# Hybrid encoder trunk: the pooled group's loads and splits as a step of their own, and the last division beside the Fourier tables

## The chip, the cores and the metric

The kernel runs on one core of a Trainium2 chip. The metric is the time of one execution in microseconds (us), as the device reports it; a kernel's figure is the median over its runs. The profile is one further execution under the hardware profiler, with a time and a span of its own.

## The reference

A trunk of two layers (DEPTH = 2) over 1040 positions (16 meta tokens ahead of 1024) and 1024 channels. Per layer:

```python
hn = rmsnorm(h, norm_w[i])
proj = einsum("bld,de->ble", hn, w_in[i])       # one projection for four head groups
y_pool = multiscale_pool(u_pool, ...) * silu(g_pool)
y_fft  = fourier_mix(u_fft, fourier_w[i]) * silu(g_fft)
y_ssd  = ssd_mixer(xbc, z, dt_raw, ...)         # bidirectional scan
y_att  = gqa_axial(q, k, v, ...) * silu(g_attn)
h = h + einsum("ble,ed->bld", concatenate([y_pool, y_fft, y_ssd, y_att]), w_out[i])
```

The pooled group is a centred mean over 2, 4, 8 or 16 positions minus the token, a linear map per group of 128 channels, a scale and the gate. The attention is softmax attention of 8 query heads on 2 key heads.

## The kernel before

Everything is kept transposed: channels on the 128 partitions, positions along the free dimension, in three chunks of 348, 346 and 346 (`CH`, line 26; in the last layer the first chunk drops the 16 meta tokens and has 332). A matrix product of full precision is three matmuls of rounded operands: `split` (lines 127 to 129) makes a high part on ScalarE and a low part on VectorE, `mm3` (lines 131 to 134) multiplies them.

**The order of the work** is written as generators. Each `yield` ends a step, and `weave` (lines 983 to 992) draws steps from several streams: each stream has a weight n, and the stream whose next step has the smallest (done + 0.5) / n goes next. So a stream with s steps and weight n ends at about s / n of the weave. The planner of the framework then makes each engine's queue from this order: it may put an instruction ahead of others where its own estimate says that its inputs and buffers are there. An engine runs its queue in that order, and so does SP, which issues nearly all transfers.

**Buffers.** `big` tiles (30 of 128 x 1056 f32, lines 97 and 98) hold nearly all that lives long; `sm("s")` is a set of four 128 x 348 tiles (lines 100 to 104) for rows on their way between DRAM and the engines. PSUM has tags "mm", "sc", "pv", "xx", and three spare banks, which `phase["spare"]` gives to one tag or another (lines 114 to 122): ('sc', 'sc', 'mm') while attention runs, ('xx', 'mm', 'xx') from the Fourier tables on. So "xx" has one bank before and three after that switch.

**Around the change** (`hybrid_trunk`, lines 1044 to 1072), once per layer:

- `att_main(l, s, t)` (line 642) is the attention of head pair t: per chunk three batches of three key blocks; `score` (line 648) makes two matmuls per head, an exponential on ScalarE and a running sum on GpSimd or VectorE (line 668); `weigh` (line 671) multiplies the batch before by the values; `divide` (line 682) sums over keys by a matmul (line 687), takes Ln and Exp, and scales (lines 691 to 693). A gate projection of 12 steps lies within. For t = 3 it has 51 steps: the last three are the last `weigh`, the last `divide`, and the gate's SiLU with product and store (lines 712 to 719).
- `pool_group` (line 357) makes the pooled rows of group g and stores them to DRAM, `s.md["p"]` (line 400): 34 steps in all.
- `fill` is a chain of projections whose results go to DRAM; at t = 3, 117 of its steps are left, the last of them those of the gate Z.
- `outproj(l, s, g, mixed, ...)` (line 330) is the output projection of head group g, 8 blocks of columns by 3 chunks, 24 steps. Its first line calls `mixed()`; for the pooled group that is `load_mixed(s, "p")` (line 320): 12 transfers through the `sm("s")` tiles (line 325), each split into `big` tiles (line 326). Each step reads the residual rows (line 338), multiplies, adds on VectorE (line 352) and stores them (line 353).
- For t = 3 the weave has three streams: attention with weight 50, the pooled groups with weight 60, and the filler with the first five out-projection steps behind it, with weight 1.5 x (108 + 5) = 169.5.
- Then the attention's pool of tiles is closed, the scan's pool is opened, and the Fourier stage begins: `fft_tables` (line 404) loads the weights `fw` (line 415; for i = 1 and 3 without their first row, so 127 rows), adds them (lines 423 and 427) and multiplies them with a cosine table (lines 432 and 434); `fft_inner` (line 443) and `fft_outer` follow. Further out-projection steps are woven in. The scan's loads (`ssd_load`, line 830, and `z` of `ssd_fin`, line 945) take tiles of the scan's pool.

Of the kernel before, what the change touches and what calls it, by code (L numbers as in the profile page):

```python
# [52 lines left out]
def hybrid_trunk(ctx: ExitStack, tc: tile.TileContext, io, out, depth=DEPTH):  # L53
# [25 lines left out]
    FB = (5, 5, 4, 1, 4, 1, 6, 9)  # L79
    GA = (22, 23, 22, 13)  # L80
    PS, WF = 60, 1.5
    FK = 3
    FN = (9, 17, 17, 16, 27)
    PC = 8 // GK
    TP = 0
# [2 lines left out]
    LS = 38  # L88
# [4 lines left out]
    def nm(s):  # L93
        uid[0] += 1
        return f"{s}{uid[0]}"

    def big(dt=F32):
        return bigp.tile([128, SLOT], dt, name=nm("big"), tag="big", bufs=NBIG)
# [3 lines left out]
    def sm(tag="n", dt=F32):  # L102
        pool = phase["p"] if tag == "q" else smp
        return pool.tile([128, 348], dt, name=nm("sm" + tag), tag="sm" + tag, bufs=phase["q"] if tag == "q" else SMB[tag])

    phase = {}
# [20 lines left out]
    def split(hi, lo, src):  # L127
        nc.scalar.copy(hi, src)  # L128
        nc.vector.tensor_tensor(lo, src, f(hi), op=ALU.subtract)  # L129
# [63 lines left out]
    def wsplit(raws, cols=128):  # L193

        r = []
        for raw in raws:
            wh = wp.tile([128, 4, 128], F32R, name=nm("wh"), tag="wh", bufs=WB[1])
            wl = wp.tile([128, 4, 128], F32R, name=nm("wl"), tag="wl", bufs=WB[1])
            split(wh[:, :, :cols], wl[:, :, :cols], raw)
            r += [(wh[:, k, :cols], wl[:, k, :cols]) for k in range(4)]  # L200
        return r

    def wraw(src, cols=128):
        w = wp.tile([128, 4, 128], F32, name=nm("wr"), tag="wr", bufs=WB[0])
        nc.sync.dma_start(w[:, :, :cols], src)
        return w[:, :, :cols]
# [109 lines left out]
    def whole(m):  # L316

        return lambda s, i, k, ci: m[i][k][:, s.ch[ci][0]:sum(s.ch[ci])]

    def load_mixed(s, key):  # L320
        m = [[big(F32R) for _ in range(4)] for _ in range(2)]
        for c0, cw in s.ch:
            for k in range(4):
                t = sm("s")
                nc.sync.dma_start(t[:, :cw], s.md[key][k, :, c0:c0 + cw])
                split(m[0][k][:, c0:c0 + cw], m[1][k][:, c0:c0 + cw], t[:, :cw])
        return whole(m)


    def outproj(l, s, g, mixed, src, dst, chunks=(0, 1, 2), pool=False, sink=None):  # L330

        part = mixed()
        for d in range(8):
            w = wsplit([wraw(io["w2"][l, g, d])])
            for ci in chunks:
                c0, cw = s.ch[ci]
                ht = sm("s")[:, :cw]
                nc.sync.dma_start(ht, src(d, ci)[:, -cw:])
                p = ps("mm")
                for k in range(4):  # L340
                    mm3(p[:, :cw], *w[k], part(s, 0, k, ci), part(s, 1, k, ci), k == 0, k == 3)
                o = ht
                if sink is not None:
                    if len(sink) == d:
                        sink.append(big())
                    o = sink[d][:, c0:c0 + cw]
                if pool:
                    t = sm("s")[:, :cw]
                    nc.scalar.copy(t, p[:, :cw])
                    nc.gpsimd.tensor_tensor(o, ht, t, op=ALU.add)  # L350
                else:
                    nc.vector.tensor_tensor(o, ht, p[:, :cw], op=ALU.add)  # L352
                nc.sync.dma_start(dst(d, ci)[:, -cw:], o)
                yield
# [623 lines left out]
    def run(*gens):  # L978
        for g in gens:
            for _ in g:  # L980
                pass

    def weave(*streams):

        st = [[iter(g), n, 0] for g, n in streams]
        while st:
            x = min(st, key=lambda x: (x[2] + 0.5) / x[1])
            x[2] += 1
            if next(x[0], StopIteration) is StopIteration:
                st.remove(x)  # L990
            else:
                yield

    def chain(*gens):
        for g in gens:
            yield from g
# [6 lines left out]
    def by_rows(x, off=0):  # L1003
        return lambda d, ci: x[d * 128:d * 128 + 128, max(CH[ci][0] - off, 0):sum(CH[ci]) - off]
# [9 lines left out]
    hsrc = by_rows(io["xT"])  # L1014
    s = layer(0)
# [7 lines left out]
    for l in range(depth):  # L1023
        last = l == depth - 1
        scope = ExitStack()
        phase["p"], phase["q"] = scope.enter_context(tc.tile_pool(name=nm("attp"), bufs=1)), 4
        phase["spare"] = SPARE[0]
        conv = iter([ssd_conv(l, s, t) for t in range(8)])
        parts = {"U": spill(l, s, T_UP, 4, "u"), "P": spill(l, s, T_GP, 4, "p", s.ch), "D": chain(spill_dt(l, s), ssd_dt(l, s)), "F": spill(l, s, T_GF, 4, "f", s.ch),
                 "Z": spill(l, s, T_Z, 4, "z", s.ch), "R": fft_proj(l, s)}  # L1030
        fill = chain(*[parts[x] if x in parts else next(conv) for x in FO])
        for g, shape in (("a", [4, 128, L]), ("p", [4, 128, L]), ("r", [4, 128, HALF + 1]), ("ny", [1, HALF + 1])):
            s.md[g] = drp.tile(shape, F32, name=nm("md"))
        s.md["x"] = drp.tile([8, 128, L], F32, name=nm("md"))
        kv = att_kv(l, s)
        if l == 0:
            run(prenorm(l, s, 0), weave((islice(kv, 2 * PC + 2), 2 * PC + 2), (prenorm(l, s, 1), 6)), weave((islice(kv, 2 * PC + 2), 2 * PC + 2), (prenorm(l, s, 2), 6)))
        else:
            run(weave((islice(kv, 4 * PC + 4), 4 * PC + 4), (prenorm(l, s, 2), 6)))
        s.h = None  # L1040
        run(weave((kv, 2 * PC + 4), (islice(fill, FK * PC), FK * PC)))
        phase["spare"] = SPARE[1]
        run(weave((chain(att_q(l, s, 0), att_max(l, s, 0)), 3 * PC + 6 + 18), (islice(fill, FN[0] * PC), FN[0] * PC)))
        for t in range(4):
            if t < 3:
                side = [att_q(l, s, t + 1), att_max(l, s, t + 1)]
            else:
                side = [pool_group(l, s, g) for g in range(4)]
            n = FN[t + 1] * PC
            if t < 3:  # L1050
                run(weave((att_main(l, s, t), LS + 3 * PC), (chain(*side), 20 + 3 * PC + 6), (islice(fill, n), n)))
        d0, d1, d2 = [hidden() for _ in range(3)]
        fill2 = chain(outproj(l, s, 0, lambda: load_mixed(s, "p"), hsrc, d0), outproj(l, s, 1, lambda: s.fm, d0, d2), outproj(l, s, 3, lambda: s.am, d2, d1, pool=True))
        run(weave((att_main(l, s, 3), LS + 3 * PC), (chain(*side), PS), (chain(fill, islice(fill2, FB[0])), WF * (n + FB[0]))))

        def stage(gen, steps, n):
            run(weave((gen, steps), (islice(fill2, n), n)))
        scope.close()
        phase["spare"] = SPARE[2]
        phase["p"], phase["q"] = scope.enter_context(tc.tile_pool(name=nm("ssdp"), bufs=1)), 3  # L1060
        tabs = fft_tables(l, s)
        next(tabs)
        run(islice(fill2, 1))
        stage(tabs, 5, FB[2] - 1)
        stage(fft_inner(l, s), 9, FB[1])
        outer = fft_outer(l, s)
        stage(islice(outer, OS[0]), OS[0], FB[3])
        s.gf = gates(s, s.gd["f"], 0, 4)
        stage(islice(outer, OS[1]), OS[1], FB[4])
        run(ssd_load(l, s))  # L1070
        stage(outer, 16 - sum(OS), FB[5])
        run(fft_mix(l, s), islice(fill2, 24 - sum(FB[:6])))
        phase["spare"] = SPARE[3]
        bwd = ssd_bwd(l, s)
        stage(islice(bwd, 4), 4, FB[6])
        s.am = load_mixed(s, "a")
        stage(bwd, 5, FB[7])
        hsrc = by_rows(out, NM) if last else hidden()
        sink = None if last else []
        tail = lambda chunks: outproj(l, s, 2, lambda: ssd_parts(s, chunks), d1, hsrc, chunks, sink=sink)  # L1080
        fwd = ssd_fwd(l, s)
        n = 48 - FB[6] - FB[7]
        stage(islice(fwd, FW), FW, n)
        run(weave((fwd, 22 - FW), (tail((0, 1)), TW)))
        scope.close()
        rest = tail((2,))
        if last:
            run(rest)
        else:
            after = layer(l + 1)  # L1090
            after.h = sink
            run(weave((rest, 8), (chain(prenorm(l + 1, after, 0), prenorm(l + 1, after, 1)), 12)))
            s = after
# [105 lines left out]
```

## Time and profile before

| | |
|---|---|
| median of 3 runs | 2157.05 us (2153.55 to 2157.64) |
| profiled execution, its own time | 2152.37 us |
| its span | 2150.6 us |
| TensorE busy in the span | 2008.4 us |
| VectorE, ScalarE, GpSimd busy | 1397.7, 1008.9, 462.6 us |
| mean granted TensorE clock | 0.97 of full speed |

Engines: PE is TensorE (PEld its weight loads), DVE is VectorE, ACT is ScalarE, POOL is GpSimd, SP the queue that issues transfers. "L132" is line 132 of the kernel; a helper's line stands for all who call it, so the tiles' names (out<-in) say which work it is: `psmm` is the PSUM tag "mm", `md` the DRAM rows of the mixed groups, `fw` the Fourier weights. A busy PE is not PE at its peak: a matmul's length is modelled, and at full clock the next one starts before it ends. PEclk is the granted clock as a share of the full 2.4 GHz.

### The profile page before, as it was taken

To read this page: it belongs to the slowest core of one execution; us is meant where nothing else is said; L and a number is where in the kernel's file an instruction comes from. 1 tells how busy PE (TensorE), PEld (TensorE's weight loads), DVE (VectorE), ACT (ScalarE), POOL (GpSimd) and SP (SyncE) were. 2 spreads that over 40 slices of the span, in tenths; PEclk is the share of its full clock that TensorE was granted. 3 is DMA by queue.
4 is the path that set the end of the run, shared out by engine and by line. 5 is a ranking of instruction groups with operands and counts; after the bars stand their busy time and mean duration, and the time that the engine had idled before them with its cause. 6 is when DMAs were issued, how large, how long until landed. Compare 5 with 4: busy or idle time off the path is not lost. (4 is left out here: it accounts for less than half of the span.)

```text
span 2150.6 us, 33395 instructions
## 1 busy us (share of the span) xinstructions
PE 2008.4 (93%) x11880; PEld 1760.3 (82%) x11880; DVE 1397.7 (65%) x2785; ACT 1008.9 (47%) x2187; POOL 462.6 (22%) x465
## 2 busy tenths in 40 slices
PE   6999999999999888988889999999999998989888
PEld 5898988689889668877779988977888995778878
DVE  5675547767664455689795754476776634466996
ACT  5535344553543346346465343436534442463662
POOL 2013122031310200245230221221312111012550
PEclk9999999999999998998999999999999999989999
DMA  4322122122323377666643221212123335776666
GB/s 140 104 66 74 52 65 60 46 76 95 99 108 119 115 202 237 194 176 190 183 128 118 66 69 50 65 53 84 66 89 102 127 107 152 211 227 183 178 185 189
DMA packets 164605, 261.01 MB, mean 121 GB/s; under 512 B 20878, under 2 KB 113618, under 8 KB 164438
## 3 DMA queue, kind: packets, MB, share of 16 engines
q1 hardware_dynamic: 161782, 249.55, 38.2%
q0 software_dynamic: 2656, 9.33, 1.8%
q8 instruction: 93, 1.52, 0.3%
q14 instruction: 74, 0.61, 0.1%
HBM read 182.91 MB, written 71.67 MB: 118 GB/s over the span
## 5 line engine op out<-in xcount | busy, mean ns | idle before, releaser
L132 PE MATMUL psmm<-big,wh 128*128 128x346 f32 (+2 forms) x1920 | 644.9, 336 | 38.5 <-ACT big L128 14.8
L133 PE MATMUL psmm<-big,wh 128*128 128x346 f32 (+2 forms) x1920 | 634.6, 331 | 6.6 <-DVE big L129 3.3
L134 PE MATMUL psmm<-big,wl 128*128 128x346 f32 (+2 forms) x1920 | 628.5, 328 | 1.3 <-DVE wl L129 1.3
L132 PEld LDWEIGHTS psmm<-big,wh 128*128 128x128 f32 x1920 | 370.9, 193 | 85.1 <-issue 32.0
L133 PEld LDWEIGHTS psmm<-big,wh 128*128 128x128 f32 x1920 | 371.4, 193 | 18.8 <-DVE big L129 6.8
L134 PEld LDWEIGHTS psmm<-big,wl 128*128 128x128 f32 x1920 | 371.5, 194 | 4.8 <-DVE wl L129 2.4
L668 POOL TENSOR_TENSOR acc<-acc,pf 116x346 f32<-116x346 f32 (+5 forms) x216 | 222.4, 1042 | 695.4 <-ACT pf L658 553.4
L128 ACT CAST wh<-wr 128x512 fp32r<-128x512 f32 (+1 forms) x236 | 145.2, 616 | 272.4 <-PE psmm L133 197.9
L129 DVE TENSOR_TENSOR wl<-wr,wh 128x512 fp32r<-128x512 f32 x232 | 168.6, 731 | 132.6 <-ACT wh L128 131.7
L132 PE MATMUL psy<-big,wh 128*128 128x346 f32 (+2 forms) x672 | 221.0, 329 | 0.8 <-ACT big L187 0.5
L133 PE MATMUL psy<-big,wh 128*128 128x346 f32 (+2 forms) x672 | 218.2, 325 | 2.7 <-DVE big L188 2.0
L134 PE MATMUL psy<-big,wl 128*128 128x346 f32 (+2 forms) x672 | 217.0, 323 | 0.0
L658 ACT ACTIVATE pf<-psy 116x346 f32<-116x346 f32 (+4 forms) x288 | 125.4, 457 | 90.2 <-PE psy L656 88.1
L678 PE MATMUL pspv<-pf,vt 116*64 116x346 f32 (+5 forms) x864 | 166.0, 466 | 0.0
L668 DVE TENSOR_TENSOR acc<-acc,pf 116x346 f32<-116x346 f32 (+5 forms) x120 | 102.2, 852 | 83.0 <-ACT pf L658 62.2
L627 DVE TENSOR_REDUCE mx<-psy 116x1 f32<-116x346 f32 (+3 forms) x272 | 132.8, 511 | 16.0 <-PE psy L626 15.4
L132 PEld LDWEIGHTS psy<-big,wh 128*128 128x128 f32 x672 | 127.0, 189 | 10.9 <-issue 6.3
L133 PEld LDWEIGHTS psy<-big,wh 128*128 128x128 f32 x672 | 127.0, 189 | 8.2 <-DVE big L188 3.1
L134 PEld LDWEIGHTS psy<-big,wl 128*128 128x128 f32 x672 | 127.2, 189 | 0.6
L678 PEld LDWEIGHTS pspv<-pf,vt 116*64 116x64 f32 (+1 forms) x864 | 58.6, 136 | 61.2 <-issue 26.8
L627 DVE TENSOR_REDUCE mx<-pssc 128x1 f32<-128x346 f32 (+3 forms) x136 | 69.8, 513 | 41.5 <-PE pssc L626 39.8
L352 DVE TENSOR_TENSOR sms<-sms,psmm 128x346 f32<-128x346 f32 (+2 forms) x104 | 52.5, 509 | 67.9 <-PE psmm L134 46.8
(290 smaller groups left out, 3376.6 us busy)
## 6 DMA issues: line engine op xcount, KB each, us to landing
wr<-w SPq DMA_DIRECT2D x248, 256.0 KB
sms<-hd SPq DMA_DIRECT2D x112, 173.0 KB
hd<-sms SPq DMA_DIRECT2D x96, 173.0 KB
bb<-csd SPq DMA_DIRECT2D x40, 338.0 KB
md<-big SPq DMA_DIRECT2D x24, 520.0 KB
gd<-sms SPq DMA_DIRECT2D x64, 173.0 KB
big<-gd SPq DMA_DIRECT2D x16, 520.0 KB
big<-md SPq DMA_DIRECT2D x16, 520.0 KB
```

Source lines behind the costliest of these rows:

```text
L128: nc.scalar.copy(hi, src)
L129: nc.vector.tensor_tensor(lo, src, f(hi), op=ALU.subtract)
L132: nc.tensor.matmul(out_ps, ah, bh, start=start, stop=False)
L133: nc.tensor.matmul(out_ps, ah, bl, start=False, stop=False)
L134: nc.tensor.matmul(out_ps, al, bh, start=False, stop=stop)
L352: nc.vector.tensor_tensor(o, ht, p[:, :cw], op=ALU.add)
L627: nc.vector.tensor_reduce(mx[:qn, q, e, ci:ci + 1], p[:qn, :cw], axis=AX.X, op=ALU.max)
L658: nc.scalar.activation(pf[:n, :cw], p[:n, :cw], AF.Exp, scale=0.125)
L668: eng.tensor_tensor(accs[c0, e][:n, :cw], accs[c0, e][:n, :cw], pf[:n, :cw], op=ALU.add)
L678: nc.tensor.matmul(hold["pv"][64 * e:64 * e + 64, :cw], s.vt[:n, k, v, :], pfs[e][:n, :cw], start=(k == 0), stop=(k == len(KTS) - 1))
```

## The change

Three things. The pooled group's `load_mixed` is a generator of its own, `early`, ahead of the out-projections: it loads and splits in its first step, and has 24 steps (`GP`); the filler stream and its weight grow by the same 24. The attention of the last head pair is cut ahead of its last two steps, so that it ends with the last `weigh`; the last division, and the SiLU with its product and store, are woven with the Fourier tables at weight 2.5. And the attention's tile pool is closed (the scan's is opened) behind the tables instead of ahead of them, while the PSUM banks are switched ahead of them, as before.

```diff
-    FK = 3
+    FK, GP = 3, 24
...
         d0, d1, d2 = [hidden() for _ in range(3)]
-        fill2 = chain(outproj(l, s, 0, lambda: load_mixed(s, "p"), hsrc, d0), outproj(l, s, 1, lambda: s.fm, d0, d2), outproj(l, s, 3, lambda: s.am, d2, d1, pool=True))
-        run(weave((att_main(l, s, 3), LS + 3 * PC), (chain(*side), PS), (chain(fill, islice(fill2, FB[0])), WF * (n + FB[0]))))
+        def early():
+
+            s.pm = load_mixed(s, "p")
+            for _ in range(GP):
+                yield
+        fill2 = chain(early(), outproj(l, s, 0, lambda: s.pm, hsrc, d0), outproj(l, s, 1, lambda: s.fm, d0, d2), outproj(l, s, 3, lambda: s.am, d2, d1, pool=True))
+        main = att_main(l, s, 3)
+        run(weave((islice(main, LS + 3 * PC - 1), LS + 3 * PC - 1), (chain(*side), PS), (chain(fill, islice(fill2, GP + FB[0])), WF * (n + GP + FB[0]))))
...
-        scope.close()
         phase["spare"] = SPARE[2]
-        phase["p"], phase["q"] = scope.enter_context(tc.tile_pool(name=nm("ssdp"), bufs=1)), 3
         tabs = fft_tables(l, s)
         next(tabs)
         run(islice(fill2, 1))
-        stage(tabs, 5, FB[2] - 1)
+        run(weave((tabs, 5), (main, 2.5), (islice(fill2, FB[2] - 1), FB[2] - 1)))
+        scope.close()
+        phase["p"], phase["q"] = scope.enter_context(tc.tile_pool(name=nm("ssdp"), bufs=1)), 3
         stage(fft_inner(l, s), 9, FB[1])
```

## Rows read from the trace of the kernel before

**Rows 1.** The page's first section: busy us, share of the span, instructions.
```profile
PE 2008.4 (93%) x11880; PEld 1760.3 (82%) x11880; DVE 1397.7 (65%) x2785; ACT 1008.9 (47%) x2187; POOL 462.6 (22%) x465
```

**Rows 2.** TensorE's waits, 580 to 830 us, then 1730 to 1880: total, times, longest.
```profile
PE psmm L132 <- ACT big L128: 6.3, 1, 6.3
...
PE psxx L687 <- DVE smn L691: 1.5, 1, 1.5
PE psxx L687 <- DVE acc L668: 1.5, 1, 1.5
...
PE psmm L132 <- ACT big L128: 6.9, 1, 6.9
...
PE psxx L687 <- DVE smn L691: 3.0, 1, 3.0
```

**Rows 3.** Windows of both layers: busy us by engine, PEclk, DMA share, GB/s.
```profile
core 0: us, PE busy (x) PEld busy (x) DVE busy (x) ACT busy (x) POOL busy (x), PEclk, DMA share, GB/s
711.00:731.00 20.00, 18.84 (x94) 11.36 (x92) 11.87 (x17) 10.96 (x27) 7.03 (x7) 1.00 0.70 208
...
737.30:745.30 8.00, 8.00 (x29) 6.49 (x29) 3.05 (x7) 0.93 (x2) 0.00 (x0) 0.63 0.32 108
...
753.70:762.40 8.70, 5.78 (x17) 4.15 (x18) 5.27 (x11) 1.46 (x4) 0.00 (x0) 0.68 0.50 146
...
1793.80:1797.90 4.10, 4.10 (x13) 2.75 (x14) 2.87 (x7) 0.92 (x2) 0.00 (x0) 0.50 0.11 40
...
1808.60:1816.50 7.90, 4.92 (x17) 2.95 (x17) 6.80 (x14) 1.40 (x3) 0.00 (x0) 0.78 0.53 142
```

**Rows 4.** TensorE's timeline, layer 0: start, length, line, operation.
```profile
711.64 1.97 PE L678 MATMUL pspv<-pf,vt 116*64 116x346 f32 x12
...
728.89 0.32 PE L655 MATMUL psy<-big,big 128*116 128x346 f32 x1
729.05 0.32 PE L656 MATMUL psy<-big,big 65*116 65x346 f32 x1
...
741.72 0.49 PE L132 MATMUL psmm<-big,wh 128*128 128x348 f32 x1
742.01 0.49 PE L133 MATMUL psmm<-big,wh 128*128 128x348 f32 x1
```

**Rows 5.** SP's timeline, layer 0; a merged row spans several transfers.
```profile
680.50 0.33 SPq L400 DMA_DIRECT2D md<-big  x1
...
710.95 0.38 SPq L325 DMA_DIRECT2D sms<-md  x1
...
722.28 0.76 SPq L415 DMA_DIRECT2D big<-fw  x2
724.71 2.27 SPq L325 DMA_DIRECT2D sms<-md  x1
...
728.99 2.22 SPq L415 DMA_DIRECT2D big<-fw  x2
```

**Rows 6.** Timelines of ScalarE and VectorE, layer 0, with the idle time before.
```profile
736.77 0.48 ACT L128 CAST big<-sms 128x346 fp32r<-128x346 f32 x1 [6.84 <-DMA sms<-md]
...
736.37 0.69 DVE L423 TENSOR_TENSOR big<-big,big 128x512 f32<-128x512 f32 x1 [7.52 <-issue]
...
749.56 0.74 DVE L423 TENSOR_TENSOR big<-big,big 128x512 f32<-128x512 f32 x1 [7.80 <-DMA big<-fw]
```

**Rows 7.** The DMA view, 700 to 760 us, in 40 slices of 1.5 us.
```profile
GB/s 0 0 119 0 0 118 0 44 318 294 269 152 110 257 297 217 186 29 146 249 272 36 25 24 24 25 25 119 333 64 25 25 24 22 174 159 227 152 70 192
```

**Rows 8.** ScalarE's timeline, layer 0: the attention gate's SiLU.
```profile
688.13 1.28 ACT L306 ACT_TABLE_LOAD   x1
689.42 1.07 ACT L306 ACTIVATE big<-big 128x1040 f32<-128x1040 f32 x1
690.51 1.28 ACT L307 ACT_TABLE_LOAD   x1
```

**Rows 9.** Timelines of SP, ScalarE and TensorE behind the tables, layer 0.
```profile
758.89 0.33 SPq L830 DMA_DIRECT2D decb<-ded  x1
...
781.02 1.28 ACT L306 ACT_TABLE_LOAD   x1 [3.69 <-DMA z<-gd]
...
784.24 0.64 PE L132 MATMUL psxx<-big,big 128*36 128x512 f32 x1 [2.42 <-ACT big L128]
```

## The prediction

> **What bounds the kernel now.** I read the page first: TensorE is busy for 93% of the span [rows 1], so time can come only from stretches in which it stands still or runs at its lower clock, and the change touches one such stretch in each of the two layers. Next I asked whom TensorE waited for there. Two kinds of wait carry nearly all of it [rows 2]: 6.3 us in layer 0 and 6.9 in layer 1 for a ScalarE split (line 128, of the pooled rows that `load_mixed` brought), and 3.0 us in each layer for the last division's matmuls (line 687). Cut by stages [rows 3], layer 0 has 20.0 us from the first load on with TensorE busy, then the wait, then 8.0 us at a mean granted clock of 0.63, and at the end 8.7 us with 2.9 idle and a clock of 0.68; layer 1 has the same shape. The clock falls to its 1.2 GHz level after each wait: matmuls start every 0.29 us instead of 0.16 [rows 4].
>
> Then the DMA queue [rows 5]. The pooled group's twelve loads start at 710.95, as the last gate projection's rows are stored. The twelfth leaves only by 726.98, behind the first two loads of the Fourier weights (line 415), and its split starts at 736.77 [rows 6], ten microseconds later. VectorE is held by the same thing: the table adds (line 423), which the planner put ahead of attention's work, wait until 736.37, and their second pair for another 7.80 us until 749.56 [rows 6]. The DMA view shows why: the core moves only 24 or 25 GB/s for five slices of 1.5 us, and soon after for three more [rows 7]. The 127-row loads (i = 1 and 3; 127 x 512 x 4 bytes are 260 KB) take 10.4 us at 25 GB/s, one after the other.
>
> **The change, part by part.** By the steps in the code, the twelve loads come directly behind the last filler projection in both versions. What moves is attention. Counting the weave, 117 filler steps at a weight of 169.5 end at 0.69 of it; at a weight of 205.5 they end at 0.57. Between the loads and the first out-projection step there were no attention steps; now there are six, with the end of a gate projection (6 matmuls at 0.16 us), four scores (16 at 0.16), one batch of weighing (12 records, 1.97 us) and a division (4 records of 0.16) [rows 4]. That is 0.96 + 2.56 + 1.97 + 0.64 = 6.1 us of TensorE work per layer. The 24 steps hold no work themselves: these 6.1 us are all the lead.
>
> First wait: if the Fourier loads leave at the same distance from the pooled loads, 6.3 (6.9) shrinks by 6.1. Bounds: 0 (the attention steps stall as well) and the whole wait. Against the full value stands ScalarE. It is busy for 10.96 of the 20 us behind the first load [rows 3], and the SiLU of the gate, 1.07 us between two table loads of 1.28, which the planner put right behind the gate projection [rows 8] and under dense filler, falls into this stretch now: 3.6 us. I take half of that off, so 4.3 per layer, 8.6 in all. The clock loss behind it is 8.0 x 0.37 = 3.0 us in layer 0 and 4.1 x 0.50 = 2.1 in layer 1 [rows 3]; bounds 0 and 5.1; I take half, because a wait of 2.42 us, later, was also followed by matmuls of 0.6 us [rows 9].
>
> Division: its matmuls leave attention's end and come behind the first table step, with three PSUM banks for "xx" instead of one, so that the waits for line 691 (which frees the one bank) and for line 668 (the last accumulation) are covered by an out-projection chunk and table matmuls. Late next is the table matmul itself: its adds go on at 749.56 at 0.74 us each [rows 6], three of them to 751.8, while TensorE came to it at the end of the last stage, 762.4 [rows 3]; were it 11 us earlier it would wait. Of 2 x 3.0 I take 4.0 (bounds 0 and 6), and of the clock there (5.78 x 0.32 and 4.92 x 0.22, together 2.9 [rows 3]) 2.0.
>
> Edits at nothing: the load of the fourth pooled row block now waits for a store issued about three steps before it instead of 30 us before (680.50 against 710.95) [rows 5]. Its 532 KB take 2.6 us at that stretch's 208 GB/s [rows 3]; between 0 and some 4 us with the landing, hidden, because the four-buffer ring spreads the loads over 16 us anyway. Only the out-projection's weights and rows stand behind it on SP; GpSimd issues no transfer there. GpSimd's accumulations for the four scores are 5 or 6 of 1.0 us [rows 3], beside 6.1 us of TensorE work; were the ring of 14 exponentials full, this would cost up to 1 us per layer.
>
> Sum: 8.6 + 2.5 + 4.0 + 2.0 = 17 us off the profiled execution's 2152.4 (span 2150.6): 2135.4. The median of the runs shown is 2157.05, 4.7 higher; runs of the new kernel will scatter likewise, so I give 2140. Upper end of the gain: 13.2 + 5.1 + 6.0 + 2.9 = 27.
>
> **A rule weighed.** The rows show the twelfth load, issued behind a 127-row load, landing with its end [rows 5, 6]. The Trainium skill, "DMA: Bandwidth & Descriptors", section "Why a DMA increments its semaphore by 16 and not by 1", says that a transfer is spread over the largest number of engines, up to 16, that divides its slowest dimension, and that 127 partitions give one. By that rule an earlier place in the program is no help to a load that leaves behind such a transfer, which speaks against this change; the trace agrees (25 GB/s), and the second rival is what it would give.
>
> **Rivals.** *Given back.* The scan stage's first loads leave once attention's buffers are free (line 830, at 758.89), and ScalarE later stands 3.69 us on the `z` load among them, ahead of the splits that the inner Fourier stage needs: 2.42 us of TensorE [rows 9]. The division now ends later against the tables by some 6 us of their matmuls, and `z` with it. Up to 6 us per layer come back: 17 - 12 = 5, so 2152. For it: `z` is on the path already. Against: the planner may put that SiLU elsewhere.
>
> *Slower.* The place is SP's order. If both 127-row loads leave ahead of the last pooled loads, the first wait ends with the second transfer, 749.56 - 736.37 = 13.2 us later [rows 6]: 6.3 + 13.2 - 6.1 = 13.4 instead of 6.3. That costs 7.1, and 2 of clock, less 3 at the division: 6 per layer, 2169. It turns on whether line 415's second pair stands before the twelfth load; now it stands behind it (728.99) [rows 5]. For it: the late store and the busier ScalarE spread the pooled loads further. Against: the Fourier tiles' buffers come free only when the gate projection ends.
>
> *All of it.* If the twelfth load leaves ahead of line 415, both waits and their clock go: 2157 - 27 = 2130.
>
> *Not what it says.* If the planner, which reorders each queue, runs the six attention steps ahead of the loads again, only the division's 6 us are left: 2151.
>
> **How the numbers follow.** Forecast 0.47 (own range 2132 to 2148), all of it 0.12, division only 0.13, given back 0.13, slower 0.15. About 0.2%, 4.3 us, is what a measurement of this kernel can tell from no change. Faster holds the first two, most of the third and part of the fourth, 0.72; the slower case gives 0.14; the rest, 0.14, is within. The range runs from 2127 (the gain's upper end, with some scatter of the medians) to 2161, which leaves out the slower case.
>
> **What would show it.** Right: line 132's longest wait for ScalarE at the first out-projection is below 3 us, line 687 has no wait at attention's end, the granted clock is near 1.0 there, and line 423 still waits for `fw` while TensorE is busy. Wrong: several line 325 loads landing late beside 25 GB/s, or a longer wait of the inner Fourier stage for ScalarE.

## The result and the profile after

| | before | after |
|---|---|---|
| median (9 runs each) | 2155.84 us (2150.33 to 2167.31) | 2136.88 us (2127.95 to 2149.78) |
| profiled execution, its own time | 2152.37 us | 2144.23 us |
| its span | 2150.6 us | 2142.5 us |

The ratio is 0.992, 95% interval 0.9892 to 0.9948: 19 us faster by the medians, 11 to 23 by the interval. The profiled execution of after is one of its longer ones, so its span shows less of the gain than the medians do. The total is close to the forecast; the way there is not.

To compare like with like I cut one stretch per layer at the same two instructions in every kernel: from the next-to-last division of head pair t = 2 (line 687) to the scan's first matmul at line 811. It holds 3275 to 3277 matmul records in both layers together, whichever kernel it is. The page's first section of after, against [rows 1]:

```profile
PE 2007.5 (94%) x11880; PEld 1756.2 (82%) x11880; DVE 1398.6 (65%) x2785; ACT 1012.6 (47%) x2191; POOL 464.2 (22%) x465
```

The windows of that stretch, layer 0 and layer 1 (columns as in [rows 3]), in the kernel before:

```profile
542.40:857.30 314.90, 293.05 (x1642) 251.93 (x1642) 170.88 (x305) 145.90 (x271) 46.01 (x42) 0.94 0.47 148
1604.10:1912.30 308.20, 284.55 (x1635) 245.72 (x1635) 166.19 (x300) 145.41 (x272) 39.74 (x42) 0.96 0.48 151
```

and in the kernel after:

```profile
544.70:849.20 304.50, 285.21 (x1641) 245.78 (x1641) 170.38 (x305) 147.52 (x274) 43.23 (x42) 0.97 0.48 153
1600.10:1902.20 302.10, 282.76 (x1635) 243.28 (x1634) 165.85 (x299) 146.02 (x269) 43.32 (x42) 0.97 0.49 153
```

The two layers together go from 623.1 to 606.6 us, -16.5, of the size of the 19. TensorE's idle time (length less busy) falls from 45.5 to 38.6, -6.9; its busy time for the same matmuls falls from 577.6 to 568.0, -9.6, with the mean granted clock up from 0.94 and 0.96 to 0.97. So in these two executions more than half of the stretch's gain is clock.

That split is one execution's. Outside the stretch (span less stretch) the same two profiles put after above before, 1535.9 against 1527.5 us, with the same idle time (96.4 and 96.7) and 8.7 us more busy time for the same work. In the 13 profiles of this study the busy time outside runs from 1426.2 to 1440.9 us. So the clock of a single execution moves a time by as much as the 9.6, and the gain as a whole rests on the medians.

TensorE's waits in the kernel after, in the two windows of [rows 2] (layer 1's cut at 1870):

```profile
PE psmm L132 <- DVE sms L352: 7.8, 1, 7.8
PE psy L132 <- ACT big L525: 4.1, 1, 4.1
PE psy L132 <- ACT big L128: 2.0, 2, 1.2
...
PE psmm L132 <- DVE sms L352: 7.5, 1, 7.5
PE psy L132 <- ACT big L128: 2.4, 4, 0.9
```

The 3.0 us at line 687 are gone in both layers. The wait of 6.3 and 6.9 us for ScalarE's split is gone too, but one of 7.8 and 7.5 us stands in its place, for VectorE at line 352 (the addition of residual rows, which frees the PSUM bank of an out-projection chunk). What stands behind it is in SP's timeline of after, layer 0:

```profile
702.07 0.38 SPq L325 DMA_DIRECT2D sms<-md  x1
...
716.22 1.28 SPq L325 DMA_DIRECT2D sms<-md  x3
717.55 5.77 SPq L415 DMA_DIRECT2D big<-fw  x3
723.42 3.28 SPq L338 DMA_DIRECT2D sms<-xT  x4
726.75 0.68 SPq L415 DMA_DIRECT2D big<-fw  x1
```

and in the timelines of VectorE and TensorE:

```profile
723.94 0.44 DVE L668 TENSOR_TENSOR acc<-acc,pf 112x346 f32<-112x346 f32 x1
732.67 1.29 DVE L423 TENSOR_TENSOR big<-big,big 128x512 f32<-128x512 f32 x2 [8.29 <-DMA big<-fw]
733.88 0.51 DVE L352 TENSOR_TENSOR sms<-sms,psmm 128x348 f32<-128x348 f32 x1
...
734.44 0.66 PE L132 MATMUL psmm<-big,wh 128*128 128x348 f32 x1 [7.77 <-DVE sms L352]
...
754.61 1.02 PE L432 MATMUL psy<-big,big 128*128 128x512 f32 x2
758.71 0.80 PE L687 MATMUL psy<-acc,ones 116*64 116x346 f32 x4
```

All twelve pooled loads (line 325) now leave ahead of the Fourier weights (line 415): the last three from 716.22, the weights from 717.55. But the planner keeps the table's sums (line 423) ahead of the residual additions (line 352) in VectorE's queue, and those sums wait for the first 127-row load until 732.67. The residual rows of the first chunks leave from 723.42, behind that load as well. So the same transfer holds TensorE, by another way. The first table matmul (line 432) comes at 754.61, where it came at 762.36 before, and the last division (line 687) runs at 758.71 without a wait. Three windows of after, where [rows 3] had ScalarE at 10.96 and the clock at 0.63 and 0.68:

```profile
702.00:722.00 20.00, 19.05 (x98) 12.39 (x98) 12.63 (x20) 17.84 (x34) 5.79 (x6) 1.00 0.61 183
...
734.00:742.00 8.00, 7.56 (x32) 6.55 (x32) 3.22 (x7) 0.95 (x3) 0.00 (x0) 0.74 0.25 88
...
752.00:762.00 10.00, 10.00 (x45) 6.24 (x43) 7.10 (x11) 3.73 (x7) 4.12 (x5) 1.00 0.40 107
```

In layer 0 the clock falls once up to the tables, behind the one long wait, and it is back at its full 2.4 GHz when they begin.

### The profile page after: what moved, and what is told of

Same layout as the page of the kernel before. It is cut to its first block, busy times and chain, and to the rows that moved or that the text cites. A ratio compares the mean times of both kernels' runs of the same rounds, so it can differ in the third digit from the quotient of the medians.

```text
span 2142.5 us, 33401 instructions
## 1 busy us (share of the span) xinstructions
PE 2007.5 (94%) x11880; PEld 1756.2 (82%) x11880; DVE 1398.6 (65%) x2785; ACT 1012.6 (47%) x2191; POOL 464.2 (22%) x465
## 4 chain that ended last, share of the span: by engine, by line
PE 68%; DVE 14%; DMA 9%; ACT 4%; issue 3%; POOL 2%; SPq 1%; DVEq 0%; POOLq 0%; ACTq 0%
PE psmm L132 11%; PE psmm L133 10%; PE psmm L134 10%; PE pspv L678 6%; PE psy L132 5%; PE psy L133 5%; PE psy L134 5%; PE psy L655 2%; PE psy L626 2%; PE psy L656 2%; DMA hd<-sms 2%; DVE bb L883 1%; PE pssc L655 1%; DMA big<-ecd 1%; PE pssc L626 1%
## 5 line engine op out<-in xcount | busy, mean ns | idle before, releaser
L668 DVE TENSOR_TENSOR acc<-acc,pf 116x346 f32<-116x346 f32 (+5 forms) x120 | 106.7, 889 | 71.5 <-ACT pf L658 51.0
L655 PE MATMUL psy<-big,big 128*116 128x346 f32 (+4 forms) x288 | 96.2, 336 | 0.9 <-DVE mx L627 0.8
```

The costliest lines, as they stand in the source:

```text
L655: nc.tensor.matmul(p[:n, :cw], k1[:, k0:k0 + n], s1[e][:, cs], start=True, stop=False)
L668: eng.tensor_tensor(accs[c0, e][:n, :cw], accs[c0, e][:n, :cw], pf[:n, :cw], op=ALU.add)
```

## The experiments

The question is what the two parts are worth, and what holds TensorE now. The theory: the end of the 127-row loads decides, whichever instruction the wait is put down to. The rivals: the added ScalarE work in the attention that is pulled out of the dense filler, or the order of the pooled loads on SP. Each run has its own kernel before beside it (medians 2155.8 to 2159.3). The last columns are the stretch above, both layers together, and TensorE's idle and busy time in it.

| run | median us | ratio, 95% interval | stretch | idle | busy |
|---|---|---|---|---|---|
| before | 2155.84 | | 623.1 | 45.5 | 577.6 |
| after | 2136.88 | 0.992 (0.9892 to 0.9948) | 606.6 | 38.6 | 568.0 |
| e1_loads_only | 2171.95 | 1.0072 (1.0054 to 1.009) | 636.7 | 57.1 | 579.6 |
| e2_division_only | 2153.64 | 0.9982 (0.9966 to 0.9998) | 621.2 | 48.3 | 572.9 |
| e3_fw128_before | 2132.27 | 0.9886 (0.9867 to 0.9904) | 597.0 | 32.4 | 564.6 |
| e4_fw128_after | 2121.73 | 0.9834 (0.9816 to 0.9852) | 584.8 | 22.7 | 562.1 |
| e5_loads_fw128 | 2136.18 | 0.9896 (0.9874 to 0.9918) | 600.8 | 33.8 | 567.0 |
| e6_division_fw128 | 2127.26 | 0.9847 (0.9822 to 0.9872) | 592.1 | 28.5 | 563.6 |
| e7_steps26 | 2145.12 | 0.9927 (0.9914 to 0.994) | 604.9 | 35.7 | 569.2 |
| e8_steps26_fw128 | 2117.53 | 0.9804 (0.9788 to 0.982) | 583.1 | 22.8 | 560.3 |
| e9_loads_fw3 | 2144.51 | 0.9946 (0.9929 to 0.9962) | 614.7 | 39.3 | 575.4 |
| e10_after_fw3 | 2137.88 | 0.992 (0.9901 to 0.9939) | 606.4 | 39.4 | 567.0 |
| e11_after_fw1 | 2118.43 | 0.9822 (0.9801 to 0.9843) | 585.9 | 20.5 | 565.4 |

**The loads' part alone.** From the kernel after, the division goes back to its old place, and the pools of tiles are switched where they were:

```diff
-        run(weave((islice(main, LS + 3 * PC - 1), LS + 3 * PC - 1), ...
+        run(weave((main, LS + 3 * PC), ...
...
-        run(weave((tabs, 5), (main, 2.5), (islice(fill2, FB[2] - 1), FB[2] - 1)))
+        stage(tabs, 5, FB[2] - 1)
```

> The loads' part alone: `early` with its 24 steps, the last division where it was. Theory A (as predicted: the lead covers the first wait): about 11 us under the kernel before, near 2145; TensorE's longest wait at the first out-projection below 3 us; line 687 keeps its 3.0 us per layer. Theory B (from the two traces: the wait only changes its name, since the 127-row loads set when VectorE goes on): a wait of 7 to 8 us per layer at the fourth out-projection chunk, for VectorE's line 352; time within 4 us of the kernel before, about 2156.

Measured: 0.72% slower than the kernel before, which neither theory had, with 11.6 us more idle time (the profiled execution, 2181.60 us, is the longest of the six). SP's timeline of this run, layer 0:

```profile
718.16 1.28 SPq L325 DMA_DIRECT2D sms<-md  x3
719.49 0.75 SPq L415 DMA_DIRECT2D big<-fw  x2
723.67 1.00 SPq L338 DMA_DIRECT2D sms<-xT  x1
724.72 1.28 SPq L415 DMA_DIRECT2D big<-fw  x2
726.10 10.60 SPq L338 DMA_DIRECT2D sms<-xT  x2
```

and the matmuls that waited:

```profile
734.95 0.66 PE L132 MATMUL psmm<-big,wh 128*128 128x348 f32 x1 [4.19 <-DVE sms L352]
746.96 0.66 PE L132 MATMUL psy<-big,wh 128*128 128x346 f32 x1 [8.08 <-DVE sms L352]
```

Here both 127-row loads leave ahead of the second chunk's residual rows (line 338), and TensorE waits for each of them in turn; layer 1 has 4.3 and 7.9. VectorE's queue has a part in the second wait: line 423 stands ahead of line 352 there and waits 9.69 us for `fw`, until 745.79. That is the prediction's slower rival, with residual rows in the place of the pooled loads. It shows also that the change's two parts can't be added up by themselves: the division's place decides where the planner puts line 338 against line 415.

**The division's part alone.** The kernel after without `early`:

```diff
-        fill2 = chain(early(), outproj(l, s, 0, lambda: s.pm, hsrc, d0), ...
+        fill2 = chain(outproj(l, s, 0, lambda: load_mixed(s, "p"), hsrc, d0), ...
```

> The division's part alone: the last division woven with the tables and the pool closed behind them, the pooled loads where they were. Theory A: 6 us under the kernel before, near 2150, with the first waits of 6.3 and 6.9 us unchanged and no wait at line 687. Theory B: most of the change's gain comes from here (the two waits at line 687, the lower clock behind them, and the wait of 2.4 and 3.5 us for the z load's SiLU), 13 to 19 us: 2137 to 2143.

Measured: 0.9982, 4 us by the ratio. The waits at line 687 are gone and busy time falls by 4.7, but idle time rises by 2.8. TensorE's waits, 580 to 850 us and then from 1720 on:

```profile
PE psmm L132 <- ACT big L128: 8.4, 2, 6.9
PE psy L132 <- ACT big L128: 5.2, 2, 4.7
...
PE psmm L132 <- ACT big L128: 7.1, 1, 7.1
PE psy L132 <- ACT big L128: 6.7, 1, 6.7
```

and ScalarE ahead of the second of them:

```profile
779.41 0.63 ACT L128 CAST big<-big 128x521 fp32r<-128x521 f32 x1 [7.45 <-DMA big<-md]
```

The first wait is the old one. The second, 4.7 and 6.7, is the inner Fourier stage, which waited 2.42 us before [rows 9] (3.5 in layer 1). TensorE comes to it sooner, at 775.4 in place of 781.8, and now the load of its first `md` rows, which leaves SP at 772.73 and which ScalarE has at 779.41, holds it. Part of the gain is given back, as that rival said, but not by its way: the `z` load leaves at 788.40 here, when that stage has begun.

**The 127-row loads made whole, in the kernels before and after.** Both kernels load all 128 rows for i = 1 and 3 and clear row 0 behind the load:

```diff
-            if i % 2:
-                nc.vector.memset(a[i][0:1], 0.0)
-            nc.sync.dma_start(a[i][i % 2:128], io["fw"][l, i, i % 2:128])
+            nc.sync.dma_start(a[i], io["fw"][l, i])
+            if i % 2:
+                nc.vector.memset(a[i][0:1], 0.0)
```

> The kernel before, with the Fourier weights i = 1 and 3 loaded as 128 rows and their first row set to zero behind the load. If the 127-row transfers are what holds the twelfth pooled load and VectorE: no wait of line 423 for fw above 2 us, the first waits of 6.3 and 6.9 us under 2 us, the waits at line 687 smaller, granted clock near 1.0 in that stretch; 17 to 24 us under the kernel before, 2132 to 2139. If the ring of four buffers or the transfer rate sets the wait: it stays above 4 us, and the time falls by less than 6 us.

> The changed kernel with the same 128-row loads. If its remaining waits (7.8 and 7.5 us at the fourth out-projection chunk) come from the 127-row transfers: they go, with their clock, about 18 us under the changed kernel, near 2119. If change and 128 rows cure the same loss: the time is that of the kernel before with 128 rows, within 5 us. If neither: within 4 us of 2137.

Measured: the kernel before gains 27 us by this edit alone (2159.19 in its own runs of before, 2132.27 with it), more than by the whole change; the kernel after gains 15 more by the medians, 19 by the ratios. In both, the long wait at line 132 goes (1.6 us is the longest left there at the out-projection). In the kernel before the edit moves the planned order as well. SP and VectorE of e3, layer 0:

```profile
724.01 0.42 SPq L413 DMA_DIRECT2D big<-fw  x1
726.53 0.32 SPq L325 DMA_DIRECT2D sms<-md  x1
726.94 0.39 SPq L413 DMA_DIRECT2D big<-fw  x1
...
732.91 0.45 DVE L352 TENSOR_TENSOR sms<-sms,psmm 128x348 f32<-128x348 f32 x1
...
734.13 1.27 DVE L423 TENSOR_TENSOR big<-big,big 128x512 f32<-128x512 f32 x2
```

The weights are loaded at line 413 there. The twelfth pooled load leaves ahead of the second weight load, and line 352 comes ahead of line 423, so the 27 us are those of the full-width load and of the order that it brings. In the kernel after the order stays where it matters. SP and VectorE of e4:

```profile
718.34 1.37 SPq L413 DMA_DIRECT2D big<-fw  x3
...
724.80 0.69 DVE L423 TENSOR_TENSOR big<-big,big 128x512 f32<-128x512 f32 x1
725.41 0.51 DVE L352 TENSOR_TENSOR sms<-sms,psmm 128x348 f32<-128x348 f32 x1
```

Three weight loads leave behind the last pooled load and ahead of the residual rows, as in the kernel after, and one of the two sums of line 423 that need the load i = 1 still stands ahead of the first line 352; it starts at 724.80 without a wait, where it started at 732.67. Layer 1 is alike. So in the kernel after the long wait is shown to be the 127-row form's. In the kernel before the form is shown to be worth 27 us, but the length of the load and the order were not tried apart. The DMA view of e3, 700 to 760 us:

```profile
GB/s 178 0 0 119 0 0 118 0 11 283 249 347 171 118 203 310 234 198 159 240 164 259 163 341 161 197 144 195 266 97 106 10 59 183 281 323 288 321 296 113
```

The Trainium skill, "DMA: Bandwidth & Descriptors", section "Why a DMA increments its semaphore by 16 and not by 1", says that 128 partitions give 16 engines where 127 give one; the runs agree, in that one row more takes the stretches at 24 and 25 GB/s of [rows 7] away.

**Each part alone, with whole loads.** The same edit in the two runs of one part.

> The loads' part alone, with the Fourier weights loaded as 128 rows. Theory C (the loads' part is slow by itself only because both 127-row transfers stand ahead of the residual rows there): the 12 us that it cost go; it is within 6 us of the kernel before with 128 rows (2132), so 2126 to 2138, and no wait for line 352 above 3 us. Theory D (the loss is attention running bare: ScalarE's table loads and splits): it stays 8 to 14 us above that kernel, 2140 to 2146.

> The division's part alone, with 128 rows. If the parts add up once the slow transfers are gone: this time and that of the loads' part with 128 rows lie as far below 2132 (the kernel before with 128 rows), summed, as the changed kernel with 128 rows does, 10.5 us; I expect most of it here, 2123 to 2128, from the waits ahead of the inner Fourier stage (3.8 and 3.4 us for ScalarE's SiLU of z). If the two parts still need each other: within 3 us of 2132.

Measured against 2132.27: the loads' part alone is 4 us slower (2136.18), the division's part 5 faster (2127.26), both together 10.5 faster (2121.73). The kernels before beside these two runs were no faster or slower than those of e3 and e4 (2159.34 and 2159.19), but the first difference is not clear of the noise: the ratios are 0.9896 and 0.9886, and their intervals overlap. So with whole loads it can't be told whether the loads' part costs anything by itself; the 0.7% that it cost with 127 rows are theirs, in the main.

The two parts need each other far less as well. By the ratios, with 127-row loads the two together are 29 us better than their sum (-17 for both, +16 and -4 alone). With whole loads it is 5 us (-11 for both, +2 and -8 alone, all against e3), and the intervals, 4 to 5 us to either side for each run, do not tell that from nothing. TensorE's waits differ so: the loads alone keep a wait of 4.8 and 3.5 us of the inner Fourier stage, the division alone waits of 4.2 and 3.4 in all for line 128's `smn`, and with both these are 1.8 and 3.1, and at most 0.9.

**26 steps instead of 24.** With 26 the planner puts the first two Fourier loads ahead of the twelfth pooled load again:

```diff
-    FK, GP = 3, 24
+    FK, GP = 3, 26
```

> The changed kernel with 26 empty steps instead of 24. Its queue on SP has the twelfth pooled load behind the first 127-row transfer again, and the fourth residual load behind the second. Theory C (where the two 127-row transfers stand in SP's queue decides): about 16 us are lost and it is near the division alone, 2147 to 2160, with a wait of 5 us or more for ScalarE's split in each layer. Theory A (the lead counts): within 4 us of the changed kernel, 2133 to 2141.

> The same 26 steps with 128 rows. Theory C: the order no longer matters and it is within 4 us of the changed kernel with 128 rows (2122), 2118 to 2126. If 26 steps are worse for another reason: 8 us or more above it.

SP and TensorE in the first of these runs, layer 0:

```profile
713.02 0.67 SPq L415 DMA_DIRECT2D big<-fw  x2
716.58 1.73 SPq L325 DMA_DIRECT2D sms<-md  x1
718.41 1.83 SPq L338 DMA_DIRECT2D sms<-xT  x3
720.29 2.08 SPq L415 DMA_DIRECT2D big<-fw  x2
...
728.36 0.66 PE L132 MATMUL psmm<-big,wh 128*128 128x346 f32 x1 [7.78 <-ACT big L128]
```

The order flipped and the wait went back to ScalarE's split at 7.8 us, as expected; the loss of some 16 us that was expected with it did not come. The ratio, 0.9927, can't be told from that of after, 0.992. (The median, 2145.12, lies between the two ranges, but the kernel before beside it was slower too, 2159.34.) So these runs show no cost of one operand over the other behind the first 127-row load. With whole loads the 26 steps have the lowest median of the study, 2117.53, 2% under the kernel before; e11 below, 2118.43, can't be told from it.

**Which of the two loads.** One of them is made whole, the other stays at 127 rows: first i = 3 alone in the run of the loads' part, then i = 3 alone and i = 1 alone in the kernel after.

```diff
-            nc.sync.dma_start(a[i][i % 2:128], io["fw"][l, i, i % 2:128])
+            nc.sync.dma_start(a[i][(i == 1):128], io["fw"][l, i, (i == 1):128])
```

(with `i == 3` in the last of the three; row 0 is cleared behind the load in each).

> The loads' part alone, as in the run that was slower than the kernel before (2172), with one edit: of the two Fourier transfers of 127 rows only the second (i = 3) is loaded as 128 rows. Theory A: the loss of the loads' part alone is its second TensorE wait (8.1 and 4.3 to 7.9 us, with the lower clock behind it, some 3 us), because residual rows stand behind both transfers. Then that wait goes, the first (4 to 8 us) stays, and the time is 2172 - 2 x 11 = 2150 (2145 to 2157), under the kernel before. Rival: the second transfer ends beside other work and the loss lies in the attention that is pulled out of dense filler; then the time stays at 2165 or above.

> The changed kernel with only the second 127-row transfer (i = 3) loaded as 128 rows. Theory A: in the changed kernel only the first 127-row transfer binds (its end sets the 7.8 and 7.5 us that TensorE waits for VectorE at line 352); the second is hidden. Then the time is that of the changed kernel, 2133 to 2141, and that wait keeps its size. Rival: each transfer is worth half of what the cure of both gave (15 us); then 2126 to 2131 and a shorter wait.

> The changed kernel with only the first 127-row transfer (i = 1) loaded as 128 rows. Theory A: this gives nearly all that the cure of both gave, 2120 to 2127, and the wait for line 352 goes. Rival: residual rows or table sums then wait for the second transfer in its place, with a TensorE wait of 5 us or more in each layer; then 2131 to 2141.

TensorE's waits in layers 0 and 1 of e9:

```profile
PE psmm L132 <- DVE sms L352: 3.7, 1, 3.7
...
PE psmm L132 <- DVE sms L352: 6.2, 1, 6.2
```

of e10, the same in both:

```profile
PE psmm L132 <- DVE sms L352: 8.3, 1, 8.3
```

and of e11, where no wait for line 352 is left:

```profile
PE psy L132 <- ACT big L525: 3.3, 1, 3.3
PE psy L132 <- ACT big L128: 2.1, 1, 2.1
...
PE psy L132 <- ACT big L525: 3.7, 1, 3.7
PE psy L132 <- ACT big L128: 2.8, 2, 2.6
```

Without the second slow load the loads' part turns from 13 us slower into 12 us faster (0.9946; the 2144.51 is half a microsecond better than the range expected), and of its two waits the second is gone. The order moves here too: in e9 the load i = 3 leaves at 722.80, behind four residual loads, where in e1 it left ahead of the second of them. In the kernel after, the second slow load costs nothing that these runs can tell (2137.88 against 2136.88), and the first is the one that counts: with it made whole, 2118.43, as good as with both. VectorE still stands for the second there:

```profile
727.75 0.52 DVE L352 TENSOR_TENSOR sms<-sms,psmm 128x348 f32<-128x348 f32 x1
736.48 2.64 DVE L423 TENSOR_TENSOR big<-big,big 128x512 f32<-128x512 f32 x3 [8.21 <-DMA big<-fw]
```

but with four residual additions ahead of that wait, and attention's last matmuls beside it, TensorE does not notice. One thing goes with the edit: in e11 the planner also puts the first additions of line 352 ahead of line 423, so the 18 us are those of the shorter load and of the order that it brings.

## Why the prediction was right, and where it was not

*The total.* 17 us were forecast and 19 measured, inside the likeliest case's own range. That it came so close is luck: the largest term had the wrong sign, and others, too small or not counted, made up for it. In the two profiles the sum reads so. First wait: 8.6 forecast, -2.1 measured (13.2 us before, 15.3 after). Division: 4.0 and 6.0. Clock: 4.5 and 9.6, with the scatter said above. Waits that the prediction put at nothing: 3.0. Together 16.5.

*First wait: wrong.* The step read "if the Fourier loads leave at the same distance from the pooled loads, 6.3 (6.9) shrinks by 6.1", and took 8.6 for both layers. The condition failed. The Fourier loads left 11.3 us behind the first pooled load before (710.95 to 722.28, [rows 5]) and 15.5 us after (702.07 to 717.55), and VectorE could go on with the end of the first 127-row load 25.4 us behind it before (736.37, [rows 6]) and 30.6 after (732.67): the transfer that the lead was meant to cover moved by 5.2 us with it. The lead itself was some 4.5 us and not 6.1: from the first pooled load to its wait TensorE had 20.05 us before (to 731.00) and 24.60 after (to 726.67). ScalarE, whose load I counted too low, empties the ring of four buffers more slowly: it was busy for 17.84 of the 20 us, with four table loads of 1.28 us, of which I had counted two; the division among the six steps brings the others. Line 415 stands behind the ring on SP. So the wait did not shrink; it is 7.8 and 7.5 us, put down to another instruction. I had also looked at the twelfth pooled load alone as what stands behind a Fourier load; the residual rows of line 338, and VectorE's own queue, stand behind it as well. The kernel after takes the first of these out and meets the next; the run with 26 steps has the first back, and a wait of the same size.

*Division: right.* All 6 us at line 687 are gone (4.0 was taken), and the first table matmul runs 7.8 us earlier in the span. What was named as late next, the table's sums, is late for VectorE alone: line 423's second pair starts at 745.48 after 6.65 us of waiting, with TensorE busy.

*Waits not counted.* The 3.0 us are a balance. Gone are the waits for line 128's `smn` (2.5 and 2.3 us before; the division's part alone keeps 4.3 and 2.8, so they go with the loads' part) and one of 3.3 us at line 793 in layer 1. The waits for line 525, 7.2 us in all before, grew by 1.6, and some of up to 1.6 us are new.

*Clock: right in kind, too small.* I took 2.5 and 2.0 us. The same matmuls take 9.6 us less, in two single executions. The prediction read the low clock in four windows next to the waits it knew; the stages behind them were under it too (in layer 0, 0.90 from 762.40 to the end of the stretch before, 0.94 from 758.70 on after). The part woven with the tables shows 4.7 us less busy time even alone (e2), where idle time rises; that is within the scatter of single executions.

*The rivals.* "All of it" had the right condition, the twelfth load ahead of line 415, and the wrong consequence. "Slower" named the mechanism that makes the loads' part alone a loss; its wrong point was to tie it to pooled loads. "Given back" happens in part where the division's part stands alone (the inner stage waits 2.3 and 3.2 us longer), but by `md` rows and not by `z`. In the full change `z` leaves late too (782.59), and ScalarE's waits for `md` are 3.97 and 3.14 us in layer 0, of which TensorE feels 2.0. Which of the three came true where depended on the order that the planner would choose, and the trace of before does not show that.

*The signs.* Two of the four signs of being right came: line 687 has no wait, and ScalarE's wait at the first out-projection is gone, though only by name. Two did not: the clock there is 0.74, and line 423's first wait for `fw` holds TensorE. The two signs of being wrong did not come either. None of them named a wait for VectorE at line 352.

*The rule weighed.* It spoke against the change, and it was the heart of the case: I used it to price a rival and did not ask what the kernel would gain if the transfer were 128 rows.

## What to carry to other kernels

Where a trace shows a stretch at a small, constant rate of transfer beside several different waits, mend the transfer before moving work about: here one row more per load, with the order that it brings, was worth 27 us, the rearrangement 19, and both with 26 steps 42. Moving work ahead to cover a load helps only if the load does not move along with it; look at the distance between the two in the queue that issues them. And where a planner writes the queues, try each part of a change alone and together: here one part was 0.7% slower, the other 0.2% faster, and the two 0.8% faster.

## What was not expected of the hardware

Idle time of TensorE costs more than its length. With whole loads in the kernel before, idle time fell by 13.1 us and the same matmuls took 13.0 us less, with the granted clock up from 0.94 and 0.96 to 0.97 and 0.98. In the kernel after the same edit gave 15.9 and 5.9, and with the first load alone 18.1 and 2.6. Over the 13 rows of the table the direction holds: the six profiles with 38 us or more of idle time have 567.0 to 579.6 us busy, the seven with less 560.3 to 569.2. How much comes back in one case can't be read from single executions, whose busy time outside the stretch alone scatters by 15 us; what sets it was not tried.
